# Seven products instead of eight in two down projections of a decoder layer, with sums of weights made in memory by GpSimd's DMA queue

## The chip, the cores and the metric

The kernel runs on one core of a Trainium2 chip. A core has five engines with queues of their own: TensorE (PE, whose weight loads are shown as PEld), VectorE (DVE), ScalarE (ACT), GpSimd (POOL) and SyncE (SP), and 16 DMA engines that move what any of them asks for. The metric is the device time of one execution in microseconds. Three runs of the kernel before took 1198.73, 1199.42 and 1199.48 us; the median is 1199.42 us.

## The reference

One step of a hybrid decoder layer on 576 tokens (512 of a prompt, 64 of eight samples), in float32, model width 1024:

```python
h = rmsnorm(x, g_pre_mix)
z = h @ w_in                          # GLA and retention heads, gates
merged = sigmoid(gate_a) * gla(z) + sigmoid(gate_b) * retention(z)
x = x + rmsnorm(merged @ w_mix_out, g_post_mix)
x = x + rmsnorm(cross_attn(rmsnorm(x, g_pre_xa), mem_k, mem_v, w_xq, w_xo), g_post_xa)
hf = rmsnorm(x, g_pre_ffn)
x = x + rmsnorm(square(relu(hf @ w_up)) @ w_down, g_post_ffn)
```

`w_up` is 1024 x 4096 and `w_down` 4096 x 1024. The states of both mixers and the keys and values of the prompt's memory are outputs too.

## The kernel before, in words

Activations lie with features on the 128 partitions and tokens along the free axis, in two halves of 288 tokens. A float32 product is made of three matmuls in a faster 32-bit type: each operand is split into a high part (ACT casts it) and a low part (DVE subtracts), and high x high, low x high and high x low are added up in PSUM (`split`, L92; `mm3`, L238; `gemm`, L243). So each weight tile of 128 x 1024 goes through a DMA of SP into `wraw` (six buffers), a cast on ACT (`wh`, L93) and a subtraction on DVE (`wl`, L94) before PE may use it; `wnext` (L226) keeps two split tiles ahead.

The program runs through: keys and values of the memory (16 weight tiles, with the first norm of x beside them, `xnorm`), eight mixer units (`mixers`), the output projection, cross attention, and the MLP in four groups of 1024 hidden features. Work that isn't a large product is written as generators in the list `side`, which `tick` advances one step after each product. A scheduler of the framework then orders each engine's instructions by its own estimates; an engine takes its instructions in that order and waits in front of each for what it needs. POOL serves the small powers of the norms (`rs`, L333 and L874), low parts of activations (`xl`, L98), and the `ks` operand of the mixers (L1063).

Group 0 of the MLP multiplies in the plain way. In groups 1 to 3 the up projection uses `sevenfold` (L273): the operands are taken as 2 x 2 quarters and combined so that seven products of quarters stand for eight (Strassen's scheme in Winograd's form). It needs sums of the quarters of x (`fsh`, `fsl`, made once by `sums_f`) and of each weight block: `begin` (L189) makes these on chip with four subtractions on DVE (L213). One product is 12 matmuls of 288 columns; four blocks of output features make a group: 4 x 7 x 12 = 336 matmuls. The down projection of all groups is plain, `gemm_m` (L250): 8 blocks x 2 halves x 8 x 3 = 384 matmuls a group, added to `y3` on DVE.

Of the kernel before, what the change touches and what calls it, by code (L numbers as in the profile page):

```python
# [13 lines left out]
P = 128  # L14
KT = 8
# [11 lines left out]


RING, STAY, RAW, SEVEN = 0, 1, 2, 3
# [29 lines left out]
def decoder_step(ctx, tc, xT, memT, ktc, vc, s_gla, s_ret, w_in, w_ga, w_a2, w_mix, w_xq, w_xk, w_xv, w_xo,  # L59
                 w_up, w_ups, w_down, vecs, cst, gam, y_out, mk_out, mv_out, sg_p, sr_p, sg_s, sr_s):  # L60
# [102 lines left out]
    def seven(w, b0):  # L163
        return [(w[b0 + b][:, kh], SEVEN) for b in range(4) for kh in range(2)]

    plan += whole(w_up) + rest(whole(w_up), 0) + whole(w_down)
    for g in range(1, 4):
        plan += seven(w_ups, 4 * (g - 1))
        plan += whole(w_down, 4 * g) + (rest(whole(w_down, 12), 0) if g == 3 else [])
    raws, ready, staying = [], [], []  # L170
    wq = []
    units = []

    def wfetch():
        if plan and sum(m == SEVEN for _, m in raws) < 2:
            src, mode = plan.pop(0), RING
            if isinstance(src, tuple):
                src, mode = src
            raw = wp.tile([P, 1024], F32, name="wraw", bufs=N_RAW)
            nc.sync.dma_start(out=raw if len(src.shape) == 2 else raw.rearrange("p (k n) -> p k n", n=src.shape[2]), in_=src)  # L180
            raws.append((raw, mode))

    def wsplit():
        if units:
            units.pop(0)()
        elif raws:
            if raws[0][1] == SEVEN:
                begin()
                return  # L189
# [4 lines left out]
            pool = staying[-1] if mode == STAY else wp  # L194
            wh = pool.tile([P, 1024], F32R, name="wh")
            wl = pool.tile([P, 1024], F32R, name="wl")
            split(wh, wl, raw)
            ready.append((wh, wl))

    def halves(w):  # L200
        return w.rearrange("p (q n) -> p q n", q=2)

    def begin():


        while len(raws) < 2:
            wfetch()
        p0, p1 = (raws.pop(0)[0] for _ in range(2))
        t = wp.tile([P, 1024], F32, name="wraw", bufs=N_RAW)
        q0, q1, qt = halves(p0), halves(p1), halves(t)  # L210

        def minus(out, a, b):
            nc.vector.tensor_tensor(out=out, in0=a, in1=b, op=ALU.subtract)  # L213

        def ring(raw):
            wh = wp.tile([P, 1024], F32R, name="wh")
            wl = wp.tile([P, 1024], F32R, name="wl")
            split(wh, wl, raw)
            ready.append((wh, wl))

        def own(raw, o, n):
            w = wq[0][:, o:o + n], wq[0][:, o + n:o + 2 * n]
            split(*w, raw)
            ready.append(w)

        def unit_a():  # L226
            ring(p0)
            wfetch()

        units.extend([unit_a, lambda: ring(t), lambda: own(p1, 0, 1024),  # L230
                      lambda: minus(q1[:, 0], q1[:, 0], qt[:, 0]), lambda: own(q1[:, 0], 2048, 512)])
# [3 lines left out]
        wfetch()  # L235

    def wnext(n=P):

        while sum(len(r) == 2 for r in ready) < 2 and (raws or plan):
            while not units and plan and len(raws) + sum(len(r) == 1 for r in ready) < N_RAW - 1:  # L240
                n0 = len(raws)
                wfetch()
                if len(raws) == n0:  # L243
                    break
            if not raws and not units:
                break
            wsplit()
# [25 lines left out]
    def sevenfold(x, p1, p5, u2, c11, c22, c12, c21):  # L273
# [11 lines left out]
        def more():  # L285
            if units:
                wsplit()

        while len(ready) < 3:
            wsplit()  # L290
# [4 lines left out]
        while units:  # L295
            wsplit()
        wd = ready.pop(0)
        prod(c, wa, 1, "S1", True)
        p5(c)
        if raws and raws[0][1] == SEVEN:  # L300
            begin()
        prod(acc, wc, 0, "S2", False)
        wsplit()
        u2(acc)
        prod(b, wb, 0, "A12", True)
        more()
        c11(b)
        prod(acc, wc, 1, "S3", False)
        c22(acc)
        prod(c, wb, 1, "S4", False)  # L310
        c12(c)
        more()
        prod(acc, wd, 0, "A22", False)
        more()
        c21(acc)
# [332 lines left out]
    xnp = ctx.enter_context(tc.tile_pool(name="xnp", bufs=2))  # L648
# [4 lines left out]
    def add(out, a, b, op=ALU.add):  # L653
        nc.vector.tensor_tensor(out=out, in0=a, in1=b, op=op)  # L654

    def sums_f():

        for j in range(4):
# [5 lines left out]
            add(c2[:, 1], c2[:, 0], c2[:, 1])  # L664
            add(c2[:, 0], c1[:, 0], c2[:, 0], ALU.subtract)
            add(c1[:, 0], c2[:, 1], c1[:, 0], ALU.subtract)
            add(c1[:, 1], c1[:, 1], c1[:, 0], ALU.subtract)
            yield
            split(fsh[:, 2:4, j], fsl[:, 2:4, j], c2)
            split(fsh[:, 0:2, j], fsl[:, 0:2, j], c1)  # L670
            yield

    FQ = {"A11": (fh, fl, 0), "A12": (fh, fl, 1), "A22": (fh, fl, 3),
          "S2": (fsh, fsl, 0), "S4": (fsh, fsl, 1), "S3": (fsh, fsl, 2), "S1": (fsh, fsl, 3)}

    def xf7(n):
        h, l, q = FQ[n]
        return h[:, q], l[:, q]

    y3 = None  # L680
    for g in range(4):
        hh = acta.tile([P, 4, 4, NH], F32R, name="hh", tag="xh")
        hl = acta.tile([P, 4, 4, NH], F32R, name="hl", tag="xl")

        if g == 0:
            lows = []
            for half in range(2):
# [14 lines left out]
                while lows:  # L702
                    lows.pop(0)()
            y3 = bigb.tile([P, KT, NT], F32, name="y3", tag="res")
            side.append(sums_f())
            wq.append(biga.tile([P, 4608], F32R, name="wq", tag="biga"))
        else:
            for b in range(4):
                c1, c2 = (hp.tile([P, 2, NH], F32, name="hr") for _ in range(2))

                def c22(ps):
                    add(c2[:, 1], ps, c2[:, 1])
                    nc.scalar.activation(c2[:, 1], c2[:, 1], AF.Relu)

                def c12(ps):
                    add(c1[:, 1], ps, c1[:, 1])
                    nc.scalar.activation(c1, c1, AF.Relu)
                    nc.scalar.activation(c1, c1, AF.Square)
                    split(hh[:, 0:2, b], hl[:, 0:2, b], c1)

                def c21(ps):
                    nc.scalar.activation(c2[:, 0], ps, AF.Relu)
                    nc.scalar.activation(c2, c2, AF.Square)
                    split(hh[:, 2:4, b], hl[:, 2:4, b], c2)

                sevenfold(xf7, lambda ps: nc.scalar.copy(c1[:, 0], ps), lambda ps: nc.scalar.copy(c2[:, 1], ps),
# [695 lines left out]
```

## Time and profile before

| what | value |
|---|---|
| median of three runs | 1199.42 us |
| the profiled execution | 1199.37 us |
| its span, first to last instruction | 1197.6 us |
| PE busy | 1168.7 us, 98% |
| DVE, ACT, POOL busy | 746.6, 563.3, 155.1 us |
| DMA, mean over the span | 131 GB/s |

The profiled execution is 1.8 us longer than its span, and 0.05 us from the median. PE is busy almost throughout; so a change counts where it takes matmuls out of PE's queue or makes PE wait. A busy share of the other engines tells only how much room they have beside PE.

### The profile page before, as it was taken

The numbers are of one execution on the slowest core, as the hardware profiler recorded it, in microseconds if no ns is written. First come the engines' busy times: TensorE is split into PE (matmuls) and PEld (weight loads), VectorE is DVE, ScalarE is ACT, GpSimd is POOL, SyncE is SP. The second block draws the span as 40 slices with busy tenths as digits, with TensorE's granted clock in tenths as the row PEclk, the third lists the DMA queues.
The fourth block names the chain that finished last, engine by engine and source line by source line (L and its number), as shares of the span: only waits on it lengthen the run. The fifth ranks groups of instructions, "written<-read, shape, count | busy, mean of one in ns | idle before, by whom it ended". The sixth has DMA issues, their size and how long they took to land.

```text
span 1197.6 us, 21977 instructions
## 1 busy us (share of the span) xinstructions
PE 1168.7 (98%) x9006; PEld 1137.6 (95%) x9006; DVE 746.6 (62%) x1332; ACT 563.3 (47%) x992; POOL 155.1 (13%) x165
## 2 busy tenths in 40 slices
PE   8899999999999999999999999999999999999995
PEld 8899999999999999999999878989999999999995
DVE  6745757465747565757868545686937546456565
ACT  5534546442445244524555434566527416515652
POOL 0522213122312222221001000000000000000000
PEclk9899999999999999999999999999999999999998
DMA  8772424242324332322644677753223223321631
GB/s 290 228 244 79 129 79 128 72 144 72 127 89 128 89 128 79 121 88 93 213 134 138 215 260 232 235 177 123 88 71 107 88 71 105 107 71 57 215 110 60
DMA packets 65621, 158.37 MB, mean 132 GB/s; under 512 B 5648, under 2 KB 34448, under 8 KB 65392
## 3 DMA queue, kind: packets, MB, share of 16 engines
q1 hardware_dynamic: 65520, 156.96, 41.0%
q8 instruction: 71, 1.16, 0.4%
q14 instruction: 30, 0.25, 0.1%
HBM read 140.68 MB, written 16.25 MB: 131 GB/s over the span
## 4 chain that ended last, share of the span: by engine, by line
PE 90%; DVE 4%; DMA 3%; issue 1%; POOL 1%; ACT 1%; SPq 0%; POOLq 0%; DVEq 0%; ACTq 0%
PE psg L251 22%; PE psg L252 22%; PE psg L253 22%; PE psa L281 6%; PE psg L281 3%; PE psa L251 2%; PE pso L281 2%; PE psa L252 1%; PE psa L253 1%; PE pso L1241 1%; DMA xf<-in_xT 1%; PE psa L1084 1%; DVE wl L94 1%; PE pso L1079 1%; DVE res L526 1%
## 5 line engine op out<-in xcount | busy, mean ns | idle before, releaser
L251 PE MATMUL psg<-xh,wh 128*128 128x288 f32 x1296 | 385.5, 298 | 0.0
L252 PE MATMUL psg<-xh,wl 128*128 128x288 f32 x1296 | 381.9, 295 | 0.8 <-DVE wl L94 0.8
L253 PE MATMUL psg<-xl,wh 128*128 128x288 f32 x1296 | 381.9, 295 | 0.0
L94 DVE TENSOR_TENSOR wl<-wraw,wh 128x1024 fp32r<-128x1024 f32 x197 | 243.4, 1236 | 89.3 <-ACT wh L93 88.5
L93 ACT CAST wh<-wraw 128x1024 fp32r<-128x1024 f32 x197 | 207.0, 1051 | 187.6 <-PE psg L253 108.2
L251 PEld LDWEIGHTS psg<-xh,wh 128*128 128x128 f32 x1296 | 243.2, 188 | 2.2 <-issue 0.8
L252 PEld LDWEIGHTS psg<-xh,wl 128*128 128x128 f32 x1296 | 243.3, 188 | 1.1 <-DVE wl L94 1.0
L253 PEld LDWEIGHTS psg<-xl,wh 128*128 128x128 f32 x1296 | 243.1, 188 | 0.1
L251 PE MATMUL psg<-hh,wh 128*128 128x288 f32 x512 | 151.2, 296 | 0.7 <-DVE y L760 0.6
L252 PE MATMUL psg<-hh,wl 128*128 128x288 f32 x512 | 151.0, 295 | 0.3 <-DVE wl L94 0.3
L253 PE MATMUL psg<-hl,wh 128*128 128x288 f32 x512 | 151.0, 295 | 0.0
L251 PEld LDWEIGHTS psg<-hh,wh 128*128 128x128 f32 x512 | 96.2, 188 | 1.6 <-issue 1.1
L252 PEld LDWEIGHTS psg<-hh,wl 128*128 128x128 f32 x512 | 96.1, 188 | 0.6 <-DVE wl L94 0.6
L253 PEld LDWEIGHTS psg<-hl,wh 128*128 128x128 f32 x512 | 96.2, 188 | 0.0
L333 POOL TENSOR_TENSOR rs<-ms,mhalf 96x3 f32<-96x3 f32 (+1 forms) x11 | 11.0, 998 | 521.5 <-DVE ms L326 521.5
L942 ACT COPY vt<-psg 128x512 f32<-128x512 f32 x16 | 9.4, 586 | 77.8 <-PE psg L253 77.8
L874 POOL TENSOR_TENSOR rs<-mv,mhalf 128x1 f32<-128x1 f32 x48 | 29.7, 619 | 112.7 <-DVE mv L869 64.6
L944 DVE COPY vd<-psg 128x128 f32<-128x128 f32 x32 | 7.8, 285 | 55.8 <-ACT vt L942 55.8
L251 PE MATMUL psg<-bh,wh 128*128 128x288 f32 x128 | 38.4, 300 | 1.6 <-ACT wh L93 1.1
L654 DVE TENSOR_TENSOR y<-psg,y 128x576 f32<-128x576 f32 x16 | 12.1, 756 | 44.2 <-PE psg L253 44.2
L252 PE MATMUL psg<-fh,wl 128*128 128x288 f32 x128 | 38.2, 298 | 0.9 <-DVE wl L94 0.9
L253 PE MATMUL psg<-fl,wh 128*128 128x288 f32 x128 | 37.9, 296 | 0.6 <-DVE fl L94 0.6
(324 smaller groups left out, 2406.2 us busy)
## 6 DMA issues: line engine op xcount, KB each, us to landing
wraw<-in_w_in SPq DMA_DIRECT2D x64, 512.0 KB, 3.7
wraw<-in_w_down SPq DMA_DIRECT2D x38, 512.0 KB, 3.7
wraw<-in_w_ups SPq DMA_DIRECT2D x24, 512.0 KB, 3.6
wraw<-in_ktc SPq DMA_DIRECT2D x16, 512.0 KB, 5.0
wraw<-in_vc SPq DMA_DIRECT2D x16, 512.0 KB, 4.4
wraw<-in_w_xq SPq DMA_DIRECT2D x14, 512.0 KB, 3.9
wraw<-in_w_xo SPq DMA_DIRECT2D x14, 512.0 KB, 5.5
wraw<-in_w_up SPq DMA_DIRECT2D x14, 512.0 KB, 4.3
```

The source lines that it names most:

```text
L93: nc.scalar.copy(hi, src)
L94: nc.vector.tensor_tensor(out=lo, in0=src, in1=f32(hi), op=ALU.subtract)
L251: nc.tensor.matmul(out, ah, bh, start=first, stop=False)
L252: nc.tensor.matmul(out, al, bh, start=False, stop=False)
L253: nc.tensor.matmul(out, ah, bl, start=False, stop=last)
L281: nc.tensor.matmul(out, s[:, q, k], m[:, k], start=first and k == i == 0, stop=k == 3 and i == 2, skip_group_check=True)
L526: nc.vector.tensor_tensor(out=res[:, kk, c], in0=y[:, kk], in1=rj, op=ALU.add)
L654: nc.vector.tensor_tensor(out=out, in0=a, in1=b, op=op)
L874: nc.gpsimd.tensor_tensor(out=rs[:t], in0=mv[:t], in1=mhalf[:t, 0:1], op=ALU.pow)
L1079: nc.tensor.matmul(so[32 * j:32 * j + 8, o], qsd[:, b * 8:b * 8 + 8], s0[:, j], start=False, stop=True, skip_group_check=True, tile_positi ...
L1084: nc.tensor.matmul(U[:, j * 256:(j + 1) * 256], kst[g][:, 2 * bp + j, :], vst[g], start=True, stop=True)
L1241: nc.tensor.matmul(acc[rows, :256], x(h), w[:, h], start=first, stop=last, skip_group_check=True, tile_position=(0, 32 * h))
```

## The change: what it does

Groups 1 and 2 of the MLP now use `sevenfold` in the down projection as well. For this the hidden activations are made as quarters and sums of quarters right after the up projection: the new function `pairs` (four DVE operations of 288 columns and two splits), called in `done21`; the plain quarters go to `ha` (split in `done1`) and into a freed part of `fh` (`done22`). Group 3 keeps its plain down projection. In `sevenfold` the product with A12 moves from the fourth place to the sixth, except in the first block of a down projection (`late`), where it is second.

The sums of the weights' quarters are no longer made on chip. They are made in DRAM while the mixers run: for each of ten pairs of weight blocks, eight transfers of 512 KB from DRAM to DRAM in POOL's queue, four copies and four that add to what is there (`sums`). The kernel then loads three quarters and four sums per block as 7 x 256 KB (`seven`), for 20 blocks.

```diff
+SUMS_AT = (2, 5, 7, 10, 12, 15, 17, 20, 22, 25)
+SUM_STEPS = (0, 0, 1, 1, 2, 3, 4, 5)
...
+    steps = {}
+    for g, at in enumerate(SUMS_AT):
+        b11, b12, b21, b22 = (w_sev[q, 2 * g:2 * g + 2] for q in range(4))
+        t1, t2, t4 = t_sev[g]
+        for n, (dst, src, plus) in zip(SUM_STEPS, (
+                (t1, b11, 0), (t2[1], b12, 0), (t1, b12, 1), (t2[1], b22, 1),
+                (t2[0], t1, 0), (t2[0], b22, 1), (t4, t2[0], 0), (t4, b21, 1))):
+            steps.setdefault(at + n, []).append((dst, src, plus))
...
+    def sums():
+        for dst, src, plus in steps.pop(clock[0], ()):
+            nc.gpsimd.dma_start(out=dst, in_=src, max_dma_last_dim=8192, **({"accum_op": ALU.add} if plus else {}))
+        clock[0] += 1
...
+    def wmore():
+
+        while plan and len(raws) < N_RAW - 1:
             wfetch()
-        p0, p1 = (raws.pop(0)[0] for _ in range(2))
...
-        minus(qt[:, 1], q1[:, 1], q0[:, 1])
-        minus(q0[:, 1], q0[:, 1], q0[:, 0])
-        minus(qt[:, 0], q1[:, 1], q0[:, 1])
-        wfetch()
+        wsplit()
...
+        def c11():
+            prod(b, wb, 0, "A12", True)
+            add(c1[:, 0], b, c1[:, 0])
+
         prod(acc, wa, 0, "A11", True)
-        p1(acc)
...
+        nc.scalar.copy(c1[:, 0], acc)
+        if late:
+            c11()
+        prod(c, wa, 1, "S1", True)
+        nc.scalar.copy(c2[:, 1], c)
+        wmore()
         wd = ready.pop(0)
...
+        prod(acc, wc, 1, "S3", False)
+        add(c2[:, 1], c2[:, 1], acc, ALU.subtract)
+        done22()
+        wmore()
+        if not late:
+            c11()
+        done1()
+        wmore()
         prod(acc, wd, 0, "A22", False)
...
+    def pairs(c1, c2, sh, sl):
+
+        add(c2[:, 1], c2[:, 0], c2[:, 1], ALU.subtract)
+        add(c2[:, 0], c1[:, 0], c2[:, 0], ALU.subtract)
+        split(sh[:, 2:4], sl[:, 2:4], c2)
+        add(c1[:, 0], c2[:, 1], c1[:, 0], ALU.subtract)
+        add(c1[:, 1], c1[:, 1], c1[:, 0])
+        split(sh[:, 0:2], sl[:, 0:2], c1)
...
+            def done1():
+                relu2(c1)
+                split(*((hh[:, 0:2, b], hl[:, 0:2, b]) if plain else (ha[:, 0, :, b], ha[:, 1, :, b])), c1)
...
+            sevenfold(xf7, c1, c2, done1, done22, done21)
+        if plain:
+            break
+        for b in range(4):
...
+            sevenfold(xh7, c1, c2, lambda: add(y[0], y[0], c1), lambda: None, done21, b == 0)
...
             for m in range(2):
                 ps = gemm_m(xh, xl)
                 sg = u2.tile([P, NT], F32, name="t2")
                 nc.scalar.activation(h2(sg), ps, AF.Sigmoid)
                 eng.tensor_tensor(out=G[:, m, :], in0=G[:, m, :], in1=sg, op=ALU.mult)
                 tick()
+            sums()
```

The scheduler does not leave the transfers in the mixers: it puts the first of them at the start of POOL's queue. These are POOL's rows from the first power of a norm (`rs`) to the second half of `xl`, in the kernel before; in brackets stands whose semaphores an instruction waits for.

```order
L333 ISA
L333 TENSOR_TENSOR rs<-ms,mhalf 128x2 [waits DVE_49]
L333 TENSOR_TENSOR rs<-ms,mhalf 96x3 [waits DVE_49]
L98 TENSOR_TENSOR xl<-xn,xh 128x288 [waits Activation_49] x8
L333 TENSOR_TENSOR rs<-ms,mhalf 96x3 [waits DVE_49,Pool_49]
```

The same place on POOL in the changed kernel, from the first instruction after the program's start; `DMASW` are the semaphores of POOL's own transfers, eight in turn, so `DMASW0` is that of the first transfer here, `DMASW1` of the second, and so on.

```order
L194 DMA t_sev<-in_w_sev 64x2048 x2
L194 DMA t_sev<-in_w_sev 64x2048 [waits DMASW0_49]
L194 DMA t_sev<-in_w_sev 64x2048 [waits DMASW1_49]
L194 DMA t_sev<-t_sev 64x2048 [waits DMASW2_49]
L194 DMA t_sev<-in_w_sev 64x2048
L329 ISA
L329 TENSOR_TENSOR rs<-ms,mhalf 128x2 [waits DVE_49]
L194 DMA t_sev<-in_w_sev 64x2048 [waits DMASW4_49]
L329 TENSOR_TENSOR rs<-ms,mhalf 96x3 [waits DVE_49]
L194 DMA t_sev<-in_w_sev 64x2048
L194 DMA t_sev<-t_sev 64x2048 [waits DMASW6_49]
L101 TENSOR_TENSOR xl<-xn,xh 128x288 [waits Activation_49] x2
```

Six transfers now stand ahead of the first `rs`, three more ahead of the first `xl`, and 18 in all by the end of `xl`; each adding transfer waits for the one that wrote its target. The other 62 follow among POOL's work of mixer units 0 to 4.

DVE's order in the memory phase moves with it. In the kernel before, around the second and third weight block; `ms`, `rs`, `dg` and `mst` are the steps of the memory's norm (`128x2`, `128x256`) and the first eviction that uses it, `ss` and `96x3` those of the first half of x.

```order
L326 TENSOR_SCALAR ms<-psa 128x2
L335 TENSOR_TENSOR dg<-idn,rs 128x256
L397 COPY mrs<-rs 128x2
L94 TENSOR_TENSOR wl<-wraw,wh 128x1024
L353 TENSOR_TENSOR ss<-ss,sq 128x576
L415 TENSOR_TENSOR mst<-psg,mbc 128x512 x2
```

The changed kernel's DVE from the same `ms` on:

```order
L322 TENSOR_SCALAR ms<-psa 128x2
L97 TENSOR_TENSOR wl<-wraw,wh 128x1024
L349 TENSOR_TENSOR ss<-ss,sq 128x576 x2
L97 TENSOR_TENSOR wl<-wraw,wh 128x1024
L349 TENSOR_TENSOR ss<-ss,sq 128x576
L318 TENSOR_TENSOR ss<-ss 128x288
L331 TENSOR_TENSOR dg<-idn,rs 128x256
L393 COPY mrs<-rs 128x2
L322 TENSOR_SCALAR ms<-psa 96x3
L411 TENSOR_TENSOR mst<-psg,mbc 128x512 x2
```

The memory's `dg` now stands behind all sums of squares of the first half of x, and its eviction `mst` behind both.

The third place is the end of an up projection on ACT, in the kernel before the last block of group 1 (`hr` are the hidden features before the split, `hh` the high part for the down projection):

```order
L713 ACTIVATE hr<-hr 128x288
L93 CAST wq<-wraw 128x1024
L717 ACTIVATE hr<-hr 128x576
L722 ACTIVATE hr<-psa 128x288
L718 ACTIVATE hr<-hr 128x576
L723 ACTIVATE hr<-hr 128x576
L93 CAST hh<-hr 128x2x288 x2
```

The same place in the changed kernel:

```order
L723 ACTIVATE hr<-hr 128x288
L724 ACTIVATE hr<-hr 128x288
L96 CAST wh<-wraw 128x1024
L96 CAST fh<-hr 128x288
L723 ACTIVATE hr<-hr 128x576
L723 ACTIVATE hr<-psa 128x288
L724 ACTIVATE hr<-hr 128x576
L724 ACTIVATE hr<-hr 128x288
L96 CAST ha<-hr 128x2x288
L96 CAST wh<-wraw 128x512
L96 CAST hh<-hr 128x2x288
```

The first product of the down projection reads `ha`, and its cast stands behind four activations.

## Rows read from the trace of the kernel before

**Rows 1.** the page's first part: busy time, share of the span, instructions

```profile
span 1197.6 us, 21977 instructions
PE 1168.7 (98%) x9006; PEld 1137.6 (95%) x9006; DVE 746.6 (62%) x1332; ACT 563.3 (47%) x992; POOL 155.1 (13%) x165
```

**Rows 2.** the page's chain that ended last, shares by engine

```profile
PE 90%; DVE 4%; DMA 3%; issue 1%; POOL 1%; ACT 1%; SPq 0%; POOLq 0%; DVEq 0%; ACTq 0%
```

**Rows 3.** busy time by stretch: up and down projections of groups 1 and 2

```profile
core 0: us, PE busy (x) PEld busy (x) DVE busy (x) ACT busy (x) POOL busy (x), PEclk, DMA share, GB/s
891.81:936.75 44.94, 44.94 (x337) 44.70 (x337) 29.68 (x39) 29.96 (x51) 0.00 (x0) 1.00 0.37 118
936.75:988.05 51.30, 51.30 (x388) 51.16 (x387) 23.97 (x28) 11.80 (x15) 0.00 (x0) 1.00 0.20 62
988.05:1032.95 44.90, 44.90 (x336) 44.66 (x336) 30.44 (x40) 29.39 (x50) 0.00 (x0) 1.00 0.38 118
1032.95:1084.29 51.34, 51.34 (x388) 51.20 (x387) 23.97 (x28) 11.83 (x15) 0.00 (x0) 1.00 0.21 62
```

**Rows 4.** the same by stretch: memory phase, its start, a stall's wake, mixers

```profile
0.00:67.00 67.00, 59.33 (x422) 56.95 (x423) 45.83 (x67) 38.53 (x63) 23.61 (x23) 0.92 0.78 257
2.00:22.00 20.00, 17.23 (x108) 16.11 (x106) 12.59 (x21) 13.09 (x23) 0.70 (x1) 0.91 0.97 354
47.80:52.20 4.40, 4.40 (x22) 4.40 (x23) 1.70 (x3) 0.26 (x1) 0.84 (x1) 0.50 0.93 256
90.00:390.00 300.00, 299.25 (x2341) 293.05 (x2340) 185.76 (x432) 138.80 (x279) 68.42 (x74) 1.00 0.34 105
704.00:708.00 4.00, 4.00 (x32) 4.00 (x31) 1.92 (x4) 2.12 (x4) 0.00 (x0) 1.00 0.93 352
```

**Rows 5.** PE's waits: for whom, us in total, times, longest

```profile
PE psa L324 <- DVE ss L322: 3.0, 1, 3.0
PE psa L1287 <- ACT osum L1283: 2.8, 1, 2.8
```

**Rows 6.** DVE in order of time, memory phase: start us, us, instruction

```profile
23.05 1.52 DVE L415 TENSOR_TENSOR mst<-psg,mbc 128x512 f32<-128x512 f32 x2
27.07 0.46 DVE L322 TENSOR_TENSOR ss<-ss 128x288 f32<-128x288 f32 x1
```

**Rows 7.** PE in order of time: the third weight block's first matmul

```profile
23.79 0.39 PE L251 MATMUL psg<-mh,wh 128*128 128x256 f32 x1
```

**Rows 8.** POOL in order of time: norms, last low part, a mixer operand

```profile
19.30 0.70 POOL L333 TENSOR_TENSOR rs<-ms,mhalf 128x2 f32<-128x2 f32 x1 [18.79 <-DVE ms L326]
64.56 1.44 POOL L98 TENSOR_TENSOR xl<-xn,xh 128x288 fp32r<-128x288 f32 x1 [0.32 <-ACT xh L97]
112.14 1.04 POOL L1063 TENSOR_TENSOR ks<-klo,cm 128x512 fp32r<-128x512 f32 x1 [6.11 <-DVE klo L1040]
```

**Rows 9.** PE in order of time: who reads that operand

```profile
114.21 0.51 PE L1084 MATMUL psa<-vs,ks 128*128 128x256 f32 x2
```

**Rows 10.** DMA issues of the memory phase: KB each, median us to landing

```profile
wraw<-in_w_xk SPq DMA_DIRECT2D x8, 512.0 KB, 7.6
```

**Rows 11.** the page's DMA issues, whole span

```profile
wraw<-in_w_in SPq DMA_DIRECT2D x64, 512.0 KB, 3.7
```

**Rows 12.** ACT in order of time, end of a block of group 1

```profile
902.60 0.69 ACT L717 ACTIVATE hr<-hr 128x576 f32<-128x576 f32 x1
903.19 0.39 ACT L722 ACTIVATE hr<-psa 128x288 f32<-128x288 f32 x1
903.48 0.68 ACT L718 ACTIVATE hr<-hr 128x576 f32<-128x576 f32 x1
904.63 1.24 ACT L93 CAST hh<-hr 128x576 fp32r<-128x576 f32 x2
```

**Rows 13.** DVE's groups by form: count, busy us, mean ns of one

```profile
L654 DVE TENSOR_TENSOR hr<-hr 128x288 f32<-128x288 f32 x16 | 7.0, 450 | 0.0
L94 DVE TENSOR_TENSOR hl<-hr,hh 128x576 fp32r<-128x576 f32 x6 | 4.3, 756 | 2.4 <-ACT hh L93 2.4
```

More of the change, by code (lines that the diff above doesn't have):

```diff
@@ L161, in decoder_step, with seven @@
     plan += rest(whole(w_xo), 0)
-    def seven(w, b0):
-        return [(w[b0 + b][:, kh], SEVEN) for b in range(4) for kh in range(2)]
+    def seven(b0):
+        out = []
+        for n in range(b0, b0 + 4):
+            g, i = n // 2, n % 2
+            b = [w_sev[q, n] for q in range(4)]
+            t1, t2, t4 = t_sev[g]
+            out += [((b[0], t1[i]), RING), ((t2[0, i], t2[1, i]), RING), ((b[2], b[3]), RING), ((t4[i],), LAST)]
+        return out
     plan += whole(w_up) + rest(whole(w_up), 0) + whole(w_down)
@@ L170, in decoder_step @@
+    clock = [0]
+    def sums():
+        for dst, src, plus in steps.pop(clock[0], ()):
+            nc.gpsimd.dma_start(out=dst, in_=src, max_dma_last_dim=8192, **({"accum_op": ALU.add} if plus else {}))
+        clock[0] += 1
     raws, ready, staying = [], [], []
-    wq = []
-    units = []
+    wdp = []
     def wfetch():
-        if plan and sum(m == SEVEN for _, m in raws) < 2:
+        if plan:
             src, mode = plan.pop(0), RING
-            if isinstance(src, tuple):
+            if isinstance(src, tuple) and isinstance(src[1], int):
@@ L683, in decoder_step, with xh7 @@
         hl = acta.tile([P, 4, 4, NH], F32R, name="hl", tag="xl")
+        plain = g in (0, 3)
+        ha = None if plain else biga.tile([P, 2, 2, 4, NH], F32R, name="ha", tag="biga")
+        def xh7(n):
+            if n in SQ:
+                return hh[:, SQ[n]], hl[:, SQ[n]]
+            return (fh[:, 2], fl[:, 2]) if n == "A22" else (ha[:, 0, n == "A12"], ha[:, 1, n == "A12"])
         if g == 0:
@@ L703, in decoder_step @@
                     lows.pop(0)()
+            xns.close()
+            wdp.append(ctx.enter_context(tc.tile_pool(name="wdp", bufs=1)))
             y3 = bigb.tile([P, KT, NT], F32, name="y3", tag="res")
             side.append(sums_f())
[L706 to L726, printed above, removed]
-                          lambda ps: nc.scalar.copy(c1[:, 1], ps), lambda ps: add(c1[:, 0], ps, c1[:, 0]), c22, c12, c21)
@@ L739, in decoder_step, with done21 @@
+        if plain:
+            break
+        for b in range(4):
+            c1, c2 = (hp.tile([P, 2, NH], F32, name="hr") for _ in range(2))
+            y = [y3[:, 2 * b:2 * b + 2, hc(half)] for half in range(2)]
+            def done21(ps):
+                nc.scalar.copy(c2[:, 0], ps)
+                add(y[1], y[1], c2)
+            sevenfold(xh7, c1, c2, lambda: add(y[0], y[0], c1), lambda: None, done21, b == 0)
     res2 = fsp.tile([P, KT, NT], F32, name="res2", tag="fsh")
@@ L1122, in unit @@
                 tick()
+            sums()
             for m in range(2):
@@ L1128, in unit @@
                 tick()
+            sums()
             def finish():
```

151 lines of the change are left out of this document (60 added, 91 removed).

## The prediction

> **What bounds the kernel now.** I read the page's first part, its chain of waits, and then busy time by stretch. PE is busy 1168.7 of 1197.6 us [rows 1], and the chain that ended last is PE for 90% [rows 2]. In the MLP there is no gap at all: in groups 1 and 2 PE is busy for the whole of the four stretches, 44.94 and 44.90 us for the up projections, 51.30 and 51.34 us for the down projections [rows 3]. Beside it ACT and DVE have room: 29.96 and 29.68 us of 44.94 in an up projection, 11.80 and 23.97 us of 51.30 in a down projection [rows 3]. The first 67 us are another thing: there PE is busy 59.33 us and the DMA engines 0.78 of the time, and from 2 to 22 us they are full, 0.97 at 354 GB/s [rows 4]. So matmuls taken away in the MLP are worth their full time, as long as nothing new is late there, and bytes added near the start go on top of a full resource.
>
> **What it removes.** A plain down projection is 384 matmuls, a seven-product one 336, as many as an up projection of the same shape. So the price of one is measured: 51.30 - 44.94 = 6.36 us in group 1 and 51.34 - 44.90 = 6.44 us in group 2 [rows 3], together 12.8 us. The four subtractions per weight block on DVE go too; DVE was not what PE waited for there, so that is worth nothing by itself.
>
> **What it adds in the MLP.** Per up block (a quarter of the stretch, 11.23 us) ACT had 29.96 / 4 = 7.5 us [rows 3]. It gets one more cast of 576 columns and one of 288, and a square of 576 becomes two of 288: about 0.6 + 0.4 + 0.3 by the starts of such activations [rows 12], so 8.8 of 11.2 us. DVE had 7.4 us; it loses four subtractions of weights and gets four of 288 columns at 0.45 us and the low parts, one of 0.756 us [rows 13] and one of half that: still under 9 us. Down blocks need less of both. So I cost the steady work at nothing; what hides it is PE's 11.2 us a block, and if ACT's order made it wait 1 us more in each of the eight up blocks, that cover would be gone and 8 us lost.
>
> The seam from an up to a down projection isn't covered. The down projection's first product reads `ha`, and its last quarter of matmuls needs the last up block's part. With E the end of that block's last matmul: the product with A12 ended 1.6 us (12 x 44.94 / 336) before E, its addition on DVE and the casts in front let the activation of 576 columns start at about E. By their spacing (0.59 us after a 576, 0.29 us after a 288) [rows 12] the four activations take until E + 1.75, the cast of `ha` until E + 2.35, its low part (0.756 us) [rows 13] until E + 3.1. PE wants the low part after 11 matmuls, at E + 1.5. It waits some 1.6 to 1.8 us; I take 1.8 us, at two seams 3.6 us. Lower bound: nothing, if A12's result is added at once. Upper bound: the clock. After a stall of 3.0 us [rows 5] PE ran at a granted 0.50 for 4.4 us [rows 4], that is 1.2 GHz and 2.2 us lost; after one of 2.8 us [rows 5] it stayed at 1.00 [rows 4]. A seam with that would cost 4 us, two 8.
>
> **What it adds at the start.** 18 of the 80 transfers stand in POOL's queue before the last `xl` (which ended at 66 us) [rows 8]. No row shows a transfer from DRAM to DRAM or one that adds. The nearest are loads of the same 512 KB: 3.7 us to landing as the median of the span [rows 11], 7.6 us in the crowded start [rows 10]. I take 5 us for quiet stages and 7 us for the start, since the start's row is of the same stage. Then POOL's own waits fit: before the first `rs` (19.30 us) [rows 8] two links of the chain must have ended, at some 16 us.
>
> But the bytes hurt. By about 20 us four transfers have written 2.1 MB, and at 354 GB/s [rows 4] that is 5.9 us of full DMA. The first half of x lands that much later, and by the new order DVE makes the memory's `dg` only after the sums of that half are done. In the kernel before the sum's last step ran at 27.07 us, and the eviction `mst`, which frees the PSUM tile for the third weight block, at 23.05 us [rows 6]; PE began that block at 23.79 us [rows 7]. Now `mst` follows the sums: 27.1 (the new order makes them sooner, the bytes later; I let the two cancel), then `dg`, its broadcast on PE, a copy, `ms` and `mst`, some 2.7 us: PE begins the third block at about 29.8 us, 6.0 us late, and its stall brings the half clock once, 2.2 us. Against that, the second half of x is now loaded ahead of the outputs that delayed it; the stall of 3.0 us behind its sums and the half clock after it (2.2 us) go: 5.2 us back. Net 8.2 - 5.2 = +3.0 us. Bounds: below, the late block costs nothing that the later stall didn't cost anyhow, -5 us; above, the DMA of the whole phase. Idle DMA up to 67 us is 0.22 x 67 = 15 us [rows 4]; 18 transfers are 9.4 MB, 27 us at 354 GB/s, up to 40 us if the adding half moves twice the bytes; so 12 to 25 us don't fit. Part of what was loaded there was weights for the next phase, which can wait; so I set the upper bound at +16 us, nearer to the lower of the two.
>
> The Trainium skill bears on this. In "DMA: Bandwidth & Descriptors", section "Issuing engines are not separate DMA queues", it says that transfers started by different engines run on the same 16 DMA engines and interleave, so a queue of GpSimd gives no bandwidth of its own; that speaks for the upper bound, 1207 us in the sum; with a path of their own the transfers would cost the start nothing, 1191 us. Rows 4 show the engines full, which is the rule's condition. The same page fits a GpSimd transfer at about 2.0 us plus its bytes at 436 GB/s; for 512 KB an estimate of 3.2 us by it, under my 5 us, and no run here shows it yet.
>
> **In the mixers** 62 transfers go between POOL's steps. DMA is at 0.34 there [rows 4], so the bytes fit: 62 x 0.524 MB are 32 MB over 300 us, about as much again as the 105 GB/s that flow. What queues behind a waiting transfer on POOL is `ks` and `rs`. The operand `ks` has the least slack: begun 112.14, 1.04 us long [rows 8], read at 114.21 [rows 9], so 1 us. Each transfer waits for one that stands two or three places before it, mostly with 5 to 10 us of other work between. At 5 us a transfer that is mostly over; I take +1 us. At 9 us, the five in a row ahead of the first `ks` would make it 1 to 2 us late, and other units likewise: up to +8 us. Below: nothing.
>
> **Sum**, against the profiled execution's 1199.37 us (its span of 1197.6 and 1.8 us around it, level with the median of 1199.42): -12.8 + 3.6 + 3.0 + 1.0 = -5.2 us, 1194.2 us. I forecast 1194 us, with a range of its own from 1191 to 1197.
>
> **The rivals.**
> *Slower by the start.* The DMA engines in the first 67 us can't carry the transfers: loads and transfers share them, each transfer takes 10 us or more, POOL reaches `rs` and `xl` late, and PE waits for the norm of x. For it: 0.97 busy from 2 to 22 us, and the 12 to 25 us that don't fit. Against it: the loads run ahead of need, and POOL holds at most about three transfers in flight. It costs +14 instead of +3: 1205 us. It decides from about +8 us at the start on (the 5.2 and the 3.0 together).
> *POOL's waits in the mixers.* Transfers take 9 us or more even at DMA 0.34, and `ks` and the powers come late in five units: +8 instead of +1, so 1201 us, and with the half clock more.
> *Nothing left.* The up blocks lose 0.7 us each to ACT's fuller order (8 of them, 5.6 us): 1199.8 us. For it: 8.8 of 11.2 us, with three copies per block that PE waits for. Against it: ACT was idle in a third of that stretch.
> *Nearly all of the gain.* The start comes out even or better (-2) because the stall at 45 us goes, and the seams cost 1 us each: -12.8 - 2 + 2 + 1, 1187.6 us.
>
> **How the numbers follow.** What a measurement can tell from no change is 0.2%, 2.4 us: faster means under 1197.0, slower over 1201.8. Chances: forecast 0.40, nearly all 0.14, nothing left 0.16, the start 0.18, the mixers 0.12. Faster takes nine tenths of the forecast and all of the second case, 0.50 rounded down to 0.48 for a mix of small costs; no change takes the third case and a little of the forecast and the mixers, 0.22; slower has the start and most of the mixers, 0.30. The range goes from 1187 (the fourth rival) to 1207 (beyond the start's 1205): left out are a better start than -2 below, and above a start at its upper bound.
>
> **What would show it.** The down stretches of groups 1 and 2 at 45 us plus a first wait of PE for `ha` of 1.5 to 2 us, twice, and no waits within up blocks. PE's largest wait moves from 45 us to the start of the third weight block, about 26 us, for a `dg` or `mst`. POOL's transfers land in about 7 us before 67 us and 5 us later; if they take 10, the start's rival holds. PE without waits from 90 to 390 us. The forecast is wrong if PE's busy time in the first 75 us falls by over 8 us, or if down stretches stay near 50.

## The result, and the profile after

The changed kernel takes 1207.96 us (median of 4 runs, 1205.94 to 1209.32) against 1199.45 us for the kernel before in the same comparison: ratio 1.0065, 95% interval 1.0048 to 1.0083, slower by 0.65%. Timed once more beside other kernels it gave 1.0075 [1.0049, 1.0100]. The forecast was 1194 us, a gain. The time lies 1 us above the top of the range, which was 1207 us.

The page of the changed kernel: its first part, the clock and DMA lines of its 40 slices (some 30 us each), and its queues (packets, MB, share of 16 engines' span).

```profile
span 1205.7 us, 22299 instructions
PE 1165.6 (97%) x8910; PEld 1133.8 (94%) x8910; DVE 761.2 (63%) x1372; ACT 596.6 (49%) x1068; POOL 203.3 (17%) x245
...
PEclk7899999999999999999999999999999999999998
DMA  9999998988433324242455577655433554554731
...
q1 hardware_dynamic: 79920, 172.69, 43.7%
q0 software_dynamic: 6400, 41.95, 13.7%
```

Against [rows 1] PE has 96 matmuls fewer and the span is 8.1 us longer. The DMA line is at 9 for the first six slices, and the clock is low in the first two. The 80 transfers (q0) cost 0.137 x 1205.7 / 80 = 2.06 us of all 16 engines each.

Where the 8.1 us come from is read by following the same instructions of VectorE through both traces. The first pair of copies of the mixers' `vd` marks the end of the start. These two rows are that pair, before, then after.

```profile
94.62 0.48 DVE L944 COPY vd<-psg 128x128 f32<-128x128 f32 x2
```

```profile
111.91 0.48 DVE L961 COPY vd<-psg 128x128 f32<-128x128 f32 x2
```

The start has lost 17.3 us. The mark is good to about 1 us: at the second pair of copies, 5 us later, the distance is 16.1 us, from 125 us on 16.9. At 370 us of the kernel before it is 16.95 us: the mixers cost nothing. At 554 us it is still 16.95, at 788 us it is 20.3 us (+3.4), and at the end 8.1 us: the MLP gave back 12.2 us. So 17.3 - 0.3 + 3.4 - 12.2, rounded, are the 8.1 us. PE up to that mark, before and after, in the columns of [rows 3]:

```profile
0.00:94.62 94.62, 86.95 (x631) 84.56 (x632) 59.05 (x86) 46.46 (x74) 30.11 (x28) 0.95 0.73 244
```

```profile
0.00:111.91 111.91, 93.69 (x640) 91.17 (x641) 60.57 (x87) 47.70 (x74) 43.59 (x54) 0.89 0.98 317
```

It stands idle 18.2 us in place of 7.7, which is 10.5 of the 17.3 us. The other 6.7 us are busy time, a few more matmuls and a lower granted clock, 0.89 in place of 0.95.

The MLP's four stretches after, in the columns of [rows 3]:

```profile
911.99:956.78 44.79, 44.79 (x339) 44.79 (x338) 33.64 (x52) 33.93 (x62) 0.00 (x0) 1.00 0.46 147
956.78:1002.23 45.45, 45.45 (x339) 44.91 (x337) 30.45 (x43) 23.63 (x39) 0.00 (x0) 1.00 0.52 163
1002.23:1047.03 44.80, 44.80 (x339) 44.80 (x337) 35.23 (x55) 33.24 (x62) 0.00 (x0) 1.00 0.52 165
1047.03:1092.48 45.45, 45.45 (x339) 44.90 (x338) 30.46 (x43) 23.64 (x39) 0.00 (x0) 1.00 0.51 163
```

The down projections went from 51.30 and 51.34 us [rows 3] to 45.45 us each; 0.66 us of that over an up projection of the same 336 matmuls is all that a seam costs. The up projections are no longer than before, with ACT at 33.9 us and DVE at 33.6 of 44.8.

The start after, by stretch as in [rows 4], with the mixers below it:

```profile
0.00:83.50 83.50, 68.54 (x463) 66.25 (x464) 48.98 (x68) 41.54 (x66) 33.44 (x42) 0.88 1.00 325
2.00:22.00 20.00, 13.85 (x74) 12.84 (x74) 8.91 (x15) 9.78 (x18) 3.25 (x6) 0.83 1.00 322
...
106.50:406.90 300.40, 299.64 (x2338) 292.82 (x2337) 186.85 (x433) 139.68 (x280) 104.45 (x131) 1.00 0.72 207
```

The DMA engines are busy for the whole of 83.5 us, where 0.78 of 67 us did before. From 2 to 22 us PE issued 74 matmuls in place of 108, at a granted clock of 0.83 in place of 0.91. The waits of PE up to 100 us, as in [rows 5], and the queues and loads up to 83.5 us, as in [rows 10]:

```profile
PE psa L338 <- DVE dg L331: 4.8, 2, 3.9
PE psg L243 <- ACT mh L382: 4.3, 1, 4.3
PE psg L243 <- DVE ga L825: 3.3, 1, 3.3
```

```profile
q1 hardware_dynamic: 8695, 18.17, 60.1%
q0 software_dynamic: 1360, 8.91, 39.6%
...
t_sev<-in_w_sev POOLq DMA_DIRECT2D x15, 512.0 KB, 8.0
wraw<-in_w_xk SPq DMA_DIRECT2D x8, 512.0 KB, 12.6
```

A load of a weight block lands after 12.6 us in place of 7.6, though it isn't a transfer of GpSimd. The rest stands behind that: PE waits 4.3 us for the memory's first operand `mh`, and the third weight block begins late. GpSimd itself isn't what is late; the two powers of the norms are asked for late by VectorE (idle time and its releaser in brackets, against [rows 8]):

```profile
26.40 0.72 POOL L329 TENSOR_TENSOR rs<-ms,mhalf 128x2 f32<-128x2 f32 x1 [8.53 <-DVE ms L322]
...
37.05 0.88 POOL L329 TENSOR_TENSOR rs<-ms,mhalf 96x3 f32<-96x3 f32 x1 [9.12 <-DVE ms L322]
```

GpSimd had stood idle, through with its transfers, for 8.5 and 9.1 us when `ms` came.

### The profile page after: what moved, and what is told of

It is laid out like the page before. It is cut to its first block, busy times and chain, and to the rows that moved or that the text cites. A ratio compares the mean times of both kernels' runs of the same rounds, so it can differ in the third digit from the quotient of the medians.

```text
span 1205.7 us, 22299 instructions
## 1 busy us (share of the span) xinstructions
PE 1165.6 (97%) x8910; PEld 1133.8 (94%) x8910; DVE 761.2 (63%) x1372; ACT 596.6 (49%) x1068; POOL 203.3 (17%) x245
## 3 DMA queue, kind: packets, MB, share of 16 engines
q0 software_dynamic: 6400, 41.95, 13.7%
## 4 chain that ended last, share of the span: by engine, by line
PE 89%; DMA 4%; DVE 4%; ACT 1%; issue 1%; POOL 1%; SPq 0%; POOLq 0%; DVEq 0%; ACTq 0%
PE psg L243 19%; PE psg L244 19%; PE psg L245 19%; PE psa L273 11%; PE psg L273 5%; PE pso L273 3%; DMA out_mv<-mst 2%; PE psa L243 2%; PE psa L244 1%; PE psa L245 1%; DMA wraw<-in_w_xk 1%; PE pso L1261 1%; PE psa L1102 1%; DVE res L522 1%; DVE wl L97 1%
## 5 line engine op out<-in xcount | busy, mean ns | idle before, releaser
L97 DVE TENSOR_TENSOR wl<-wraw,wh 128x1024 fp32r<-128x1024 f32 x237 | 285.0, 1203 | 115.4 <-ACT wh L96 112.2
L96 ACT CAST wh<-wraw 128x1024 fp32r<-128x1024 f32 x237 | 240.2, 1014 | 135.5 <-PE psg L245 46.9
L243 PE MATMUL psg<-hh,wh 128*128 128x288 f32 x256 | 76.1, 297 | 0.7 <-DVE y L776 0.6
L244 PE MATMUL psg<-hh,wl 128*128 128x288 f32 x256 | 75.4, 295 | 0.3 <-DVE wl L97 0.3
L245 PE MATMUL psg<-hl,wh 128*128 128x288 f32 x256 | 75.4, 295 | 0.0
L243 PEld LDWEIGHTS psg<-hh,wh 128*128 128x128 f32 x256 | 48.1, 188 | 1.2 <-issue 1.1
L194 POOL DMA_DIRECT2D t_sev<-in_w_sev x60 | 43.9, 754 | 30.7 <-DMA t_sev<-t_sev 16.4
L244 PEld LDWEIGHTS psg<-hh,wl 128*128 128x128 f32 x256 | 48.0, 188 | 0.6 <-DVE wl L97 0.6
L245 PEld LDWEIGHTS psg<-hl,wh 128*128 128x128 f32 x256 | 48.0, 188 | 0.2 <-DVE hl L97 0.2
L349 DVE TENSOR_TENSOR ss<-ss,sq 128x576 f32<-128x576 f32 x34 | 25.7, 755 | 22.4 <-ACT sq L348 22.4
```

The source lines that it names most:

```text
L96: nc.scalar.copy(hi, src)
L97: nc.vector.tensor_tensor(out=lo, in0=src, in1=f32(hi), op=ALU.subtract)
L194: nc.gpsimd.dma_start(out=dst, in_=src, max_dma_last_dim=8192, **({"accum_op": ALU.add} if plus else {}))
L243: nc.tensor.matmul(out, ah, bh, start=first, stop=False)
L244: nc.tensor.matmul(out, al, bh, start=False, stop=False)
L245: nc.tensor.matmul(out, ah, bl, start=False, stop=last)
```

## The experiments

The main theory after the result: **bytes**. The transfers and the loads share the 16 DMA engines, these are overfull, and the start lasts as long as their work. Its rivals: the **order** (the memory's `dg` behind the sums of x), and **GpSimd's waits** in its queue. The kernels were compared in three groups, of four, four and three, the second on another chip than the first and third; each ratio is to the kernel before in that comparison, whose median was 1199.5 to 1201.3 us.

**No transfers.** In `sums()` the transfer is left out, and `seven()` loads plain quarters:

```
-            nc.gpsimd.dma_start(out=dst, in_=src, ...)
+            pass
-        out += [((b[0], t1[i]), RING), ((t2[0, i], t2[1, i]), RING), ((b[2], b[3]), RING), ((t4[i],), LAST)]
+        out += [((b[0], b[1]), RING), ((b[2], b[3]), RING), ((b[2], b[3]), RING), ((b[2],), LAST)]
```

> The changed kernel without its 80 transfers in GpSimd's queue. The loads of the MLP read plain quarters where they read sums, with the same number of bytes; so the sums of weights' quarters are left out of what is computed, and no other work. Theory 1 (bytes: the transfers overfill the DMA engines in the first 75 us): the start falls back to its old length and only the MLP's gain is left. The down stretches of groups 1 and 2 took 45.45 us each in the changed kernel against 51.30 and 51.34 before, so about 1199.4 - 12 = 1187 us, or up to 1191 if the half clock that cost 3.4 us between 580 and 790 us comes back. Rival (the MLP's change itself costs something elsewhere, and the start is only half of the loss): 1194 or more.

Measured: 1188.48 us, ratio 0.9905 [0.9891, 0.9920]. The first `vd` stands where it stood before:

```profile
94.64 0.48 DVE L961 COPY vd<-psg 128x128 f32<-128x128 f32 x2
```

So the MLP's gain is real and whole, and all of the start's loss hangs on the transfers. This alone doesn't part bytes from order, since without transfers the scheduler also kept the order of the kernel before.

**A quarter and a half of the bytes.** The plain loads as above, and in `sums()`:

```
-            nc.gpsimd.dma_start(out=dst, in_=src, ...)
+            nc.gpsimd.dma_start(out=dst[0, :64], in_=src[0, :64], ...)     # a quarter; half: dst[:1], src[:1]
```

> The changed kernel with each of the 80 transfers cut to a quarter of its bytes (128 KB, same places in GpSimd's queue, same chain of waits; order of PE, DVE and ACT as in the changed kernel). The loads of the MLP read plain quarters, so the sums are left out of what is computed. Theory 1 (bytes): the kernel before kept the DMA engines busy for 52 of the first 67 us; in the changed kernel 19 transfers took 33 us of them. A quarter of that is 8 us, which fits into the 15 idle us: the start costs 0 to 2 us and the time is 1188 to 1192. Theory 2 (order: the norm of the memory is made behind the sums of x, the third weight block starts late whatever the bytes): start +6 to +10, 1193 to 1198. Theory 3 (GpSimd stands waiting in its queue, and with it the norm's power and the low parts): a transfer of a quarter still takes half as long or more, so at least half of the 16.5 us stays, 1196 or more.

> The same with half of the bytes in each transfer (256 KB); the sums are left out of what is computed. Theory 1 (bytes): 52 + 17 = 69 us of DMA for a phase of 67: it is just full, the start costs 3 to 6 us, and the time is 1190 to 1196; the cost is far from half of the whole one since the idle 15 us are used first. Theory 2 (order): as with a quarter, 1193 to 1198 in both. Theory 3 (waits in GpSimd's queue): between the quarter and the whole, 1199 to 1203.

Measured: 1192.19 us, 0.9937 [0.9921, 0.9952] for the quarter, 1194.01 us, 0.9949 [0.9928, 0.9970] for the half. The first `vd` of the quarter, and its GpSimd queue up to 69 us:

```profile
96.45 0.48 DVE L961 COPY vd<-psg 128x128 f32<-128x128 f32 x2
```

```profile
q0 software_dynamic: 544, 2.23, 15.8%
```

The same of the half, its queue up to 72 us:

```profile
99.70 0.48 DVE L961 COPY vd<-psg 128x128 f32<-128x128 f32 x2
```

```profile
q0 software_dynamic: 790, 4.38, 26.7%
```

All three doses have the same order on PE, ACT and DVE and the same chain of waits in GpSimd's queue, and cost 1.8, 5.1 and 17.3 us at that mark. The kernel before used 0.78 x 67 = 52 us of the engines in 67 us [rows 4]. With the quarter's 0.158 x 69 = 10.9 us that makes 63: it fits, and 1.8 us are left for the order. With the half's 0.267 x 72 = 19.2 us it makes 71 us, 4 more than 67; with the whole 0.396 x 83.5 = 33.1 us it makes 85 us, 18 more. The cost isn't in proportion to the bytes: it begins where the idle time is used up, and from there each us of transfers is about a us of the kernel. The order is worth no more than the quarter's 1.8 us. GpSimd's waits for transfers are shorter there, but not by much, in the first 67 us of the quarter and the first 83.5 of the whole:

```profile
POOL t_sev L194 <- DMA t_sev<-in_w_sev: 9.1, 3, 4.2
```

```profile
POOL t_sev L194 <- DMA t_sev<-in_w_sev: 12.6, 3, 6.0
```

So 9.1 us of such waits go with a loss of 1.8 us, and 3.5 us more of them don't explain one of 17.3. What no run here parts is the 16 engines from the memory behind them: a busy share doesn't tell what holds the packets up.

The quarter shows the order by itself. `mst`, which frees the tile for the third weight block, ran there at

```profile
30.47 1.27 DVE L411 TENSOR_TENSOR mst<-psg,mbc 128x512 f32<-128x512 f32 x2
```

against 23.05 us [rows 6], so that block is late by 7.4 us, near the 6.0 forecast, and nearly all of it is made good later, as the prediction had it.

**Copies in place of adding transfers.**

```
-   nc.gpsimd.dma_start(out=dst, in_=src, max_dma_last_dim=8192, **({"accum_op": ALU.add} if plus else {}))
+   nc.gpsimd.dma_start(out=dst, in_=src, max_dma_last_dim=8192)
```

> The changed kernel with copies in place of the adding transfers: same bytes, same order on all engines; the additions are left out of what is computed. Theory 1 (an adding transfer takes no more of the DMA engines than a copy; all cost 2 us of the 16 engines per 512 KB): 1206 to 1210, as the changed kernel. Theory 2 (adding takes more, since it reads what it adds to): the share of GpSimd's queue falls from 13.7% to 11% or less, and the start costs 8 to 12 us in place of 16.5, 1199 to 1204.

Measured: 1199.26 us, 0.9983 [0.9968, 0.9997]; GpSimd's queue over the span, the same up to 74 us, and the first `vd`:

```profile
q0 software_dynamic: 6400, 41.95, 10.1%
```

```profile
q0 software_dynamic: 1294, 8.50, 30.7%
```

```profile
102.67 0.48 DVE L961 COPY vd<-psg 128x128 f32<-128x128 f32 x2
```

The same packets and bytes take 10.1% of a span of 1197.7 us in place of 13.7%: 1.51 us of 16 engines for a copy, so, half of the 80 being of each kind, 2 x 2.06 - 1.51 = 2.6 us for one that adds. The 2.6 us are an estimate: they take a copy to cost the same in both kernels. The start costs 8.0 us; 52 + 0.307 x 74 = 75 us say 8.

**Transfers from 30 us on.** An edge for the scheduler, without a semaphore, behind the second norm's power:

```
+        powers.append(nc.gpsimd.tensor_tensor(out=rs[:t, :n], in0=ms, in1=mhalf[:t, :n], op=ALU.pow))
...
+            move = nc.gpsimd.dma_start(out=dst, in_=src, ...)
+            tc.add_manual_dep(move.ins, powers[1].ins.name, ..., reason="place")
```

> The changed kernel with its whole computation; the same kind of edge keeps all transfers behind the power of x's first half (rs), which ran at 28.5 us in the kernel before. 13 transfers instead of 19 are left ahead of the last low part of x, and the order of PE at the start is that of the kernel before. Theory 1 (the bytes of the whole phase count): 13 transfers by 1.95 us are 25 us of the 16 engines; between 30 and 67 us the kernel before left 10 us idle; so the start is still 8 to 15 us longer, 1196 to 1204. Theory 2 (only the loads of the first 30 us matter: memory and x; later loads run ahead of need): 0 to 3 us, 1188 to 1192.

Measured: 1203.76 us, 1.0022 [1.0008, 1.0036], and the first `vd` 7.8 us late:

```profile
102.39 0.49 DVE L963 COPY vd<-psg 128x128 f32<-128x128 f32 x2 [1.40 <-ACT vt L961]
```

Here the memory and the first half of x come undisturbed, the order is the old one up to 35 us, and GpSimd waits for none of its transfers in the first 90 us; yet nearly half of the loss stays. So neither those first loads nor GpSimd's waits are needed for it. It comes at one place: up to 80.3 us PE has done 522 matmuls, in the kernel before 523. Then it stands still (PE, ACT, then the stores `out_mv` of the memory's values: min, median and longest time to landing, here and in the kernel before):

```profile
86.74 0.61 PE L245 MATMUL psg<-xh,wh 128*128 128x288 f32 x1 [6.41 <-DVE ga L827]
84.57 0.62 ACT L822 CAST a2s<-t 96x512 fp32r<-96x512 f32 x1 [12.25 <-DMA out_mv<-mst]
DMA to landing us min/median/max: 8.1/8.6/14.5
```

```profile
DMA to landing us min/median/max: 3.2/4.4/6.4
```

The last store, issued at 70.04 us, lands after 14.5 us, in the kernel before after 6.4. ACT's `a2s` waits for it, the eviction `ga` stands behind that, and PE behind `ga`. The weights loaded beside it, `wraw<-in_w_in`, landed after 11.8 us in place of 4.7, and no wait of PE of over 1 us is put down to them: they could wait, the store at the stage's end could not. The balance has to be drawn from 30 us on: there 0.26 x 37 = 9.6 us were idle and the transfers take 0.409 x 45 = 18.4, so 8.8 don't fit; over the whole stage it would be 3.7.

**Transfers in the mixers.** Three ways to keep all of them out of the start. First, a small transfer of a tile that the mixers make goes ahead of each group's first two:

```
+        if any(first for *_, first in now):
+            nc.vector.tensor_copy(gate[0:1], made[0:1, 0:8])
+            if first:
+                nc.gpsimd.dma_start(out=dst[0, 0:1, 0:8], in_=gate[0:1])
```

> The changed kernel with the whole of its computation, but each group's first two transfers wait for a tile that the mixers make at the place in the code where they stand (a small transfer of that tile into the same memory goes ahead), so no transfer runs in the first 100 us. Theory 1 (bytes at the start): the start has its old length, the order there is that of the kernel before, and 1187 to 1191 us are left. Rival (the bytes cost the same wherever they are; POOL's steps in the mixers stand behind their waits): the mixers from 100 to 390 us become 6 us longer or more, 1194 to 1200.

Measured: 1198.10 us, 0.9986 [0.9971, 1.0002], not to be told from the kernel before: the rival's time. The start is as before, but from 95 to 600 us GpSimd stands 120 us in its queue for transfers, and PE waits for what follows the norms behind it (waits of POOL, then the longest of PE in total):

```profile
POOL t_sev L201 <- DMA t_sev<-in_w_sev: 88.0, 27, 6.9
...
POOL t_sev L201 <- DMA t_sev<-t_sev: 32.6, 13, 4.9
```

```profile
PE psa L1129 <- DVE on L903: 2.4, 3, 1.0
```

Second, the scheduler's edge from the instruction that stands ahead of each `sums()` call in the code (`add_manual_dep(move.ins, made.ins.name, ...)`); third, the same edge from the mixers' first instruction of GpSimd for all (`begun = nc.gpsimd.memset(f32(sp[g]), 0.0)`).

> The changed kernel with its whole computation; an edge for the scheduler (no semaphore) keeps each of the 80 transfers behind the mixers' instruction of VectorE or GpSimd that stands ahead of it in the code. So none runs before 100 us, as in the gated kernel, but each also stands some 12 us behind the one that it waits for. In the gated kernel GpSimd stood 120 us in its queue for transfers, with the norms' powers (rs) behind it, and PE waited six times about 1 us for what follows. Theory 1 (that loss is GpSimd's waits in its queue): they are gone here, the mixers lose under 2 us, 1188 to 1191 us. Rival (the bytes of 80 transfers beside the mixers' own loads cost it, by whatever order): as the gated kernel, 1194 to 1199.

> The changed kernel with its whole computation; the edge keeps all transfers behind GpSimd's first instruction of the mixers (76 us in the kernel before), and from there on they may run as early as the scheduler likes, as they do in the changed kernel. Theory 1 (all of the start's loss is bytes beside the loads up to 67 us, and the mixers bear the transfers in that dense order, as they did in the changed kernel, where they lost 0.4 us): 1187 to 1191. Rival (dense transfers make GpSimd late for ks and the powers now that nothing was done ahead of them): 1193 to 1199, as the gated kernel.

Measured: own places 1194.34 us, 0.9944 [0.9922, 0.9967]; after the memory phase 1191.64 us, 0.9925 [0.9909, 0.9941]. Both beat the kernel before; their intervals overlap. GpSimd's waits for transfers from 95 to 600 us fell from 120 to 46 and 51 us, not to nothing. From 121 to 522 us of the kernel before, the same 3135 matmuls in each trace, the stage grew by 8.9 us in the gated kernel, 5.3 in the second and 2.6 in the third, and PE stands idle there 5.4, 2.3 and 0.7 us; so idle time is only a part of it, and what the rest is stays open. One profile of each doesn't rank them: in a second profile of the third (below) the stage grew by 6.9 us, with 3.3 us idle. The third's DMA engines from 95 to 300 us, in its first profile and its second, and last those of the changed kernel from its mark on:

```profile
95.00:300.00 205.00, 203.54 (x1581) 198.75 (x1580) 122.83 (x288) 93.94 (x188) 83.22 (x108) 1.00 0.95 260
```

```profile
95.00:300.00 205.00, 200.95 (x1549) 195.86 (x1548) 118.83 (x279) 91.79 (x183) 82.50 (x107) 0.99 0.93 255
```

```profile
111.00:300.00 189.00, 188.24 (x1464) 183.81 (x1464) 115.48 (x267) 87.79 (x174) 75.85 (x101) 1.00 0.92 260
```

The changed kernel has 0.92 over 189 us with PE busy 188.2, and the stage grew by 0.8 and 0.9 us in its two profiles. So full engines cost nothing by themselves where the stage's own loads need 0.34 of them [rows 4]; the second profile of the third shows that they can go with a loss.

**Repeats.** Three kernels ran once more.

> The kernel before once more, for its profile alone. Between 580 and 790 us the changed kernel fell 3.4 us further behind than the start explains: PE's granted clock was 0.91 in two stretches there, behind waits (1.6 us at 582, 3.0 us for osum at 716) that the kernel before also has, at 1.00. No transfer runs there any more. Theory 1 (whether the clock falls behind such a wait differs from execution to execution, whatever the kernel): this profile may show it in none, one or two of the places; any fall here shows that it isn't the change. Theory 2 (the change causes it): 1.00 in both places, as in the first profile, and 1.00 cannot be told from chance by this run alone.

> The changed kernel once more, for a second profile and times. The start's loss comes from what is in flight and should repeat: first copy of v (vd) in the mixers at about 116 us, DMA at 1.0 until then. Between 580 and 790 us, theory 1 (by execution): another loss than 3.4 us, anything from 0 to 6; theory 2 (the change causes it): 3 to 4 us again, at the same two places.

> The kernel whose transfers all stand behind the memory phase (as in the run after_memory), timed in more rounds. If its gain is what was measured (ratio 0.9925, the MLP's 12 us less 1 to 2 us in the mixers), the ratio lies between 0.990 and 0.994 again; if the first result was a lucky chip, 0.995 or more.

Measured: the kernel before 1202.44 us (one run); the changed one 1.0075, its first `vd` at 112.32 us, as the first time and not at the 116 expected; after the memory phase 1192.04 us, 0.9923 [0.9908, 0.9938], as the first time. Two stretches of the changed kernel behind which most of the 3.4 us lie, the first with two waits, of 0.5 and 1.1 us:

```profile
587.00:607.00 20.00, 18.42 (x127) 17.96 (x126) 17.64 (x21) 12.83 (x20) 0.56 (x1) 0.91 0.60 195
708.40:728.60 20.20, 17.17 (x138) 15.27 (x138) 7.74 (x10) 6.76 (x10) 1.08 (x2) 0.92 0.78 265
```

The first of these in the kernel before, in its first profile and in the second:

```profile
570.00:590.00 20.00, 18.42 (x136) 17.55 (x134) 18.17 (x22) 12.93 (x20) 0.60 (x1) 1.00 0.62 195
```

```profile
570.00:590.00 20.00, 18.43 (x126) 17.83 (x125) 17.31 (x21) 12.49 (x20) 0.57 (x1) 0.91 0.59 193
```

The same kernel with the same two waits (18.4 us busy of 20) kept its clock once and lost it once, and its second profile is 3.3 us longer between 580 and 790 us. So a loss of this size there needs no change. In the changed kernel's second profile this stage lost 6.6 us, 3.2 more than in its first; over the profiles of all kernels it lost between nothing (gated) and 6.6 us. Whether the changed kernel's mean is higher than that of the kernel before stays open.

## Why the prediction was wrong, step by step

**What it removes: right.** 12.8 us for 96 matmuls; the down projections fell by 5.85 and 5.89 us, the rest, 1.1 us, is the seams.

**The seams: too dear.** 1.8 us each forecast, 0.66 measured. The working had PE wait at the twelfth matmul of the down projection. The order has the three matmuls that read the last block's part of `ha`, its low part last, behind the start of the product with A12, which fills the time (PE of the changed kernel, first seam):

```profile
957.98 0.29 PE L273 MATMUL pso<-ha,wh 128*128 128x288 f32 x1
...
959.32 0.40 PE L273 MATMUL psa<-ha,wh 128*128 128x288 f32 x1
...
960.49 0.33 PE L273 MATMUL psa<-ha,wh 128*128 128x288 f32 x1
```

The accumulation into `psa` is left open at 957.98 and closed at 960.49. With the steady up blocks at no cost, which held, the MLP gave 12.2 us, not 9.2.

**The start: this step failed.** It was put at +3.0 us, as one late weight block (+8.2) less a recouped stall (-5.2), with the bytes entered once, as a delay of x's first half that was let cancel against an earlier sum. Measured: +17.3 us. The mechanism that was costed exists and is worth 1.8 us, in the quarter. What was left out of the value, and stood in the upper bound, is the balance of the whole phase: "12 to 25 us don't fit" was right. It was set aside because "part of what was loaded there was weights for the next phase, which can wait". Some of it could, as the transfers from 30 us on showed; but the memory's and x's loads and the stores run on the same engines and could not, and PE waits for what hangs on them: `mh` 4.3 us, `dg` 4.8, `ga` 3.3. The last step of x's sums ran at 34.79 us, not 27.1, and the third block began at 37.61, not 29.8:

```profile
34.79 0.46 DVE L318 TENSOR_TENSOR ss<-ss 128x288 f32<-128x288 f32 x1
```

```profile
37.61 0.58 PE L243 MATMUL psg<-mh,wh 128*128 128x256 f32 x1 [0.84 <-DVE mst L411]
```

In the changed kernel the transfers took 33 us of the engines and 15 were idle [rows 4]: 18 us don't fit, the middle of the 12 to 25 that the prediction had worked out, and the start is 17 us longer. The 7 us taken for a transfer there to land were 8.0 for those from an input.

The rule that was weighed there held: the Trainium skill, "DMA: Bandwidth & Descriptors", section "Issuing engines are not separate DMA queues". GpSimd's queue took 39.6% of the same engines, and SyncE's loads slowed from 7.6 [rows 10] to 12.6 us; the sum by that rule was 1207 us, the time is 1207.96. That they agree to 1 us is partly luck: the sum has 3.6 us for the seams, which cost 1.3, and nothing for the 3.4 us between 580 and 790 us. The same page's fit for one transfer, the estimate of 3.2 us, isn't what happened under load: 8.0 us to landing.

**The mixers: right for the changed kernel**, +1 forecast, between -0.3 and 0.8 measured by the mark that is taken; with some luck, since the 5 us taken for a transfer to land were 8.0 there, the median of the 42 that read an input (in the gated kernel PE did wait for norms that stood behind transfers, as that rival had it). **The named rival** "slower by the start" had the place, the sign and 1205 us. Of its links, the full engines held, and so did PE's waits for the norms (`dg`); the transfers took 8.0 us, not 10 or more, and "POOL reaches `rs` and `xl` late" didn't hold for `rs`: GpSimd waited for VectorE. The forecast gave this rival 0.18 although [rows 4] showed 0.97 from 2 to 22 us.

**Of the signs** the down stretches at 45 us came true, but PE has no wait for `ha` there. The sign named to refute was set too high: PE's busy time in the first 75 us fell by 7.3 us, from 67.33 to 60.04, short of the 8; the rest of the loss is half clock (a granted 0.93 in this stretch before, 0.86 after) and what came behind it. Each row: the first 75 us, before and after.

```profile
0.00:75.00 75.00, 67.33 (x483) 64.94 (x484) 47.46 (x68) 40.31 (x66) 23.61 (x23) 0.93 0.80 266
```

```profile
0.00:75.00 75.00, 60.04 (x396) 57.75 (x397) 43.91 (x62) 37.43 (x59) 28.86 (x37) 0.86 0.99 329
```

The count says it better: 87 matmuls fewer by then. Busy time hides a slower clock; the count of matmuls doesn't.

## What to carry to other kernels

Before adding transfers to a stage, balance its DMA engines from the first transfer to the end of the stage: busy share times length, plus the transfers' own engine time, against the length. In this start what exceeded it was lost one for one, and what fitted was nearly free. Look also for what must have landed before the next stage can begin; here that was a store. A transfer without a dependency goes where the scheduler likes, not where it stands in the code; one edge for the scheduler (here behind the memory phase) turned a loss of 0.65% into a gain of 0.75%, though it didn't keep the mixers free of loss in every execution. And the price of an operation that no row shows should be entered at both ends in the stage's balance, not only in its range.

## What the runs showed of the hardware that was not expected

- A transfer from DRAM to DRAM of 512 KB took 1.51 us of the 16 DMA engines as a copy and, by an estimate from the two kernels' shares, about 2.6 us as one that adds, with the same packets and bytes in the records.
- DMA engines at 0.92 for 189 us left PE busy 188.2 us in the mixers of the changed kernel; at 1.00 for 83.5 us they went with a loss of 17 us in its start. The stages' own loads needed 0.34 and 0.78.
- With the engines at 1.02 of their time from 30 to 75 us, a store of 256 KB took 14.5 us to landing in place of 6.4, and PE stood idle 6.4 us behind it.
- After the same two waits, 0.5 and 1.1 us, the granted clock was 1.00 in one execution of the kernel before and 0.91, part of the 20 us at 1.2 GHz, in another.
